# Last stage of a one-layer encoder trunk: the remaining operand splits issued in the fifth pass, and the additions of x to the u3 blocks on VectorE

## Chip, cores and metric

The kernel runs on one NeuronCore of a Trainium2 chip. The metric is the device time of one execution in microseconds; the median of several runs counts.

## What is computed

The reference is one layer of an encoder trunk on x (1024 frames of 1024 features, f32): a mixer, a SwiGLU feed-forward, and a last stage that adds a gated embedding. Only the last stage is touched by the change:

```python
h3 = rmsnorm(x, norm_ple_g[li])
x = x + jax.nn.sigmoid(h3 @ w_ple_gate[li]) * (p[li].astype(x.dtype) @ w_ple_proj[li])
```

The kernel holds everything transposed: features on the 128 partitions, frames along the free axis, in eight tiles of 128 x 1024. The embedding product `p @ w_ple_proj` was made much earlier and lies in DRAM.

## The kernel before

**Arithmetic.** Every f32 operand of a matrix product is split into a rounded part hi and a rest lo; a product is three matmuls (hi·hi, hi·lo, lo·hi). A split of a 128 x 1024 operand is an ACT copy (hi, a cast) and a subtraction on DVE (lo). Weights are split in the same way by ACT (line 123) and, in this stage, by GpSimd (POOL, line 126), which is fed by a DMA into `wr`.

**The seven passes.** The 1024 x 1024 product of the last stage, with `w_ple_gate`, is done by a Strassen scheme with seven half-size products, in the order of `KINDS`: A11, S2, A12, S3, S1, A22, S4 (lines 964 and 965 name the weight, the operand and the chain of each). A pass has four steps (`k`), and in each step 4 output blocks (`u`) of 128 x 512 take three matmuls. The passes accumulate in three chains of four PSUM banks: x (A11, A12), y (S2, S3, A22) and z (S1, S4). After a pass `after(kind, u, ps)` combines the banks. The seventh pass, S4, goes block by block instead: all its matmuls for one `u`, then `last` for that block; the fourth block is cut into two halves of 256 columns, and `last` is called for both halves after the matmuls of both have been issued, so that both waits count up to the very last matmul.

**The end of an output block.** `out(c, h, t, add)` is a stream of four parts for one block: DVE multiplies by the row factors `rb`; ACT takes the sigmoid; DVE multiplies by the embedding block `e`; and the engine `add` (GpSimd unless told otherwise) adds x, after which a DMA stores the block. `some(n)` moves streams on by one part each, so that four blocks go through a part together.

**Operand splits.** The fourteen operand tiles are split one by one with `m_split` in the order `m_order`. `operand`, called in the first and third step of a pass, takes the next split pair from `m_ready` and calls `m_split` when fewer than two are left: so the two T4 operands of the sixth pass are split during the fifth, and the two B22 operands of the seventh pass during the sixth. `side` is a generator that `passes` moves on once after each step; it holds the loads of the embedding blocks and the work on the output blocks.

**Order on an engine.** All operations through `self.V`, `self.A` and `self.G` are pinned to the order of the code on DVE, ACT and POOL; each engine takes its instructions in that order, and one that waits holds up those behind it. The weight copies (line 123) and weight rests (line 126) are not pinned: a scheduler at build time places them.

**Names.** `pm_13973` to `pm_13976` are the banks of chain z (blocks u = 0 to 3), `pm_13715` to `pm_13718` those of chain y, `s_13597` and `s_13598` hold the four u3 blocks (two in each), `s_13863` and `s_13864` the embedding blocks of the same columns, `rb_13622` the row factors. The operation that makes an output block of u3 final (fifth pass, S1) is `V.tensor_tensor(u3[u], ps, u3[u], ALU.add)`; the one beside it, `V.tensor_tensor(ps, ps, u2[u], ALU.add)`, prepares the bank for S4. The two together, for four blocks, are called the eight z additions below.

Of the kernel before, what the change touches and what calls it, by code (L numbers as in the profile page):

```python
# [56 lines left out]
class Trunk:  # L57
# [1650 lines left out]
    def ple(self):  # L1708
        nc, V, A, G = self.nc, self.V, self.A, self.G
        h0, h1 = slice(0, HALF), slice(HALF, T)  # L1710
        p1, u2, u3 = [[t[:, h] for t in (self.slot(), self.slot()) for h in (h0, h1)] for _ in range(3)]
        es = {}

        def load(odd, h):
            tiles = [self.slot() for _ in range(2)]
            for u in range(4):
                e = es[2 * u + odd, h.start] = tiles[u // 2][:, u % 2 * HALF:u % 2 * HALF + HALF]
                self.load(e, self.es[2 * u + odd][:, h])

        todo = []  # L1720

        def out(c, h, t, add=G, sp=None):

            sp = sp or slice(0, HALF)
            t, e = t[:, sp], es[c, h.start][:, sp]
            at = slice(h.start + sp.start, h.start + sp.stop)
            V.tensor_tensor(t, t, self.rb[:, at], ALU.mult)
            yield
            A.activation(t, t, AF.Sigmoid)
            yield  # L1730
            V.tensor_tensor(e, t, e, ALU.mult)
            yield
            add.tensor_tensor(e, e, self.x[c][:, at], ALU.add)
            nc.sync.dma_start(self.out[c][:, at], e)

        def some(n):

            for stream in todo[:n]:
                next(stream, None)

        def after(kind, u, ps):
            if kind == "A11":
                A.copy(p1[u], ps)
            elif kind == "S2":
                V.tensor_tensor(ps, ps, p1[u], ALU.add)
                A.copy(u2[u], ps)
            elif kind == "A12":
                todo.append(out(2 * u, h1, ps))
                next(todo[-1])
            elif kind == "S3":  # L1750
                A.copy(u3[u], ps)
            elif kind == "S1":
                V.tensor_tensor(u3[u], ps, u3[u], ALU.add)
                V.tensor_tensor(ps, ps, u2[u], ALU.add)
                todo.append(out(2 * u + 1, h0, u3[u]))
            elif kind == "A22":
                todo.append(out(2 * u + 1, h1, ps))
                next(todo[-1])
                next(todo[-1])

        def last(u, ps, sp):
            for _ in range(max(0, min(2, len(todo) - u))):
                drain(todo.pop(0))
            stream = out(2 * u, h0, ps, V, sp)
            next(stream)
            next(stream)
            todo.append(stream)
            if 0 < u < 3:
                drain(todo.pop(0))

        def operand(b, i):
            got = self.m_ready.pop(0)
            if len(self.m_ready) < 2:
                self.m_split()
            return got

        def side():
            self.half_sums(0)
            for k in range(4):
                self.square(self.x[2 * k][:, h1], 1)  # L1780
            yield
            self.half_rows(0)
            for k in range(2):
                self.ple_part("B21", k, False)
            yield
            self.half_sums(1)
            for k in range(2, 4):
                self.ple_part("B21", k, False)
            yield
            self.half_rows(1)  # L1790
            yield
            m = self.m
            load(0, h1)
            yield
            for i in range(2):
                m["T1", i] = self.slot()
                V.tensor_tensor(m["T1", i], m["B22", i], m["T2", i], ALU.subtract)
                yield
            yield

            for i in range(2):
                V.tensor_tensor(m["T2", i], m["B21", i], m["T2", i], ALU.subtract)
                m["T4", i] = m["T2", i]
                yield
            load(1, h0)
            yield
            yield
            for i in range(4):
                some(4)
                yield  # L1810
            del todo[:]

            load(1, h1)
            for i in range(4):
                yield
            load(0, h0)
            for i in range(4):
                some(4)
                if i == 3:
                    del todo[:4]  # L1820
                yield

        yield from self.passes(4, operand, after, side(), last)
        while todo:
            drain(todo.pop(0))
# [94 lines left out]
def drain(stream):  # L1920
    while True:
        try:
            next(stream)
        except StopIteration as e:
            return e.value
# [114 lines left out]
```

## Time and profile before

| | us |
|---|---|
| three runs | 1594.68, 1595.65, 1601.39 |
| median | 1595.65 |
| the profiled execution, its time | 1595.63 |
| its span, first to last instruction | 1593.7 |
| PE busy in the span | 1566.2 (98%) |
| DVE busy | 1171.8 (74%) |
| POOL busy | 783.6 (49%) |
| ACT busy | 643.7 (40%) |

PE is TensorE's matmul row, DVE is VectorE, ACT is ScalarE, POOL is GpSimd, SP is the engine that issues the DMAs. The mean granted TensorE clock was 0.998. The profiled execution lies within 0.02 us of the median, and its time is 1.93 us above its span. Instructions of a queue overlap: an instruction's duration is longer than the distance to the start of the next one, so that the distance between starts (called the pitch below) is what one instruction costs a busy queue. Times in the rows are counted from the start of the span.

### The profile page before, as it was taken

What the parts mean: (1) busy time and instruction counts of PE and PEld (TensorE: products, weight loads), DVE (VectorE), ACT (ScalarE), POOL (GpSimd) and SP (SyncE); (2) the same over time, 40 slices, a digit from 0 to 9 for tenths busy, and PEclk for the clock granted to TensorE, in tenths of its full rate; (3) what the DMA queues carried; (4) which work ended last, traced back from release to release, by engine and by line L of the source; (5) the groups of instructions that cost most, each with busy time, mean ns of one, the idle gap of its engine ahead of it and who ended that gap; (6) DMA issues with size and microseconds to landing.
All of it is one profiled execution on the core that took longest, in us unless ns stands there. A gap on an engine that the chain in (4) does not pass through costs nothing.

```text
span 1593.7 us, 21834 instructions
## 1 busy us (share of the span) xinstructions
PE 1566.2 (98%) x8224; PEld 1309.3 (82%) x8224; DVE 1171.8 (74%) x1767; ACT 643.7 (40%) x1089; POOL 783.6 (49%) x445
## 2 busy tenths in 40 slices
PE   8999999999999999999999999999999999999997
PEld 6998989877888888888887788888888888888886
DVE  5656765489998777544898988888888866765658
ACT  5321221167677633421377322232222234445453
POOL 3422221257563064325230777777777764644554
PEclk9999999999999999999999999999999999999999
DMA  5101100245663465475244422233333268875334
GB/s 191 54 28 41 40 28 27 100 146 174 224 245 107 143 192 187 146 285 210 80 141 177 152 99 99 100 99 109 103 108 108 80 255 322 304 278 189 126 134 157
DMA packets 81897, 230.52 MB, mean 145 GB/s; under 512 B 9216, under 2 KB 9984, under 8 KB 81280
## 3 DMA queue, kind: packets, MB, share of 16 engines
q1 hardware_dynamic: 81648, 229.12, 40.6%
q8 instruction: 64, 1.05, 0.2%
q14 instruction: 41, 0.34, 0.1%
q10 hardware_dynamic: 144, 0.02, 0.0%
HBM read 163.82 MB, written 65.27 MB: 144 GB/s over the span
## 4 chain that ended last, share of the span: by engine, by line
PE 80%; DVE 9%; POOL 2%; ACT 2%; issue 2%; DMA 1%; SPq 0%; POOLq 0%; ACTq 0%; DVEq 0%
PE pm L83 77%; DVE s L54 5%; PE pm L86 2%; DVE m L54 2%; ACT s L54 1%; POOL wl L126 1%; POOL m L556 1%; DVE q L54 0%; DVE wl L126 0%; ACT wh L123 0%; DVE pm L54 0%; DMA d<-s 0%; DMA s<-in_oq 0%; POOL s L1075 0%; DMA wr<-d 0%
## 5 line engine op out<-in xcount | busy, mean ns | idle before, releaser
L83 PE MATMUL pm<-s,wh 128*128 128x512 f32 (+1 forms) x1712 | 532.1, 392 | 6.7 <-ACT wh L123 5.2
L83 PE MATMUL pm<-s,whi 128*128 128x512 f32 x1568 | 488.1, 392 | 1.2 <-DVE t L54 1.2
L126 POOL TENSOR_TENSOR wl<-wr,wh 128x1024 fp32r<-128x1024 f32 (+2 forms) x108 | 265.0, 2460 | 395.9 <-ACT wh L123 392.6
L83 PEld LDWEIGHTS pm<-s,wh 128*128 128x128 f32 x1712 | 320.1, 189 | 73.7 <-ACT wh L123 5.2
L83 PEld LDWEIGHTS pm<-s,whi 128*128 128x128 f32 x1568 | 294.7, 188 | 67.0 <-DVE t L54 1.7
L83 PE MATMUL pm<-s,wl 128*128 128x512 f32 (+1 forms) x856 | 334.1, 390 | 0.0
L54 DVE TENSOR_TENSOR s<-s,s 128x512 f32<-128x512 f32 (+4 forms) x213 | 257.3, 1236 | 90.5 <-ACT s L54 53.1
L83 PE MATMUL pm<-s,wlo 128*128 128x512 f32 x784 | 307.9, 393 | 0.9 <-DVE wlo L54 0.5
L83 PE MATMUL pm<-wh,s 128*128 128x256 f32 (+1 forms) x896 | 238.2, 340 | 0.0
L123 ACT CAST wh<-wr 128x1024 fp32r<-128x1024 f32 (+2 forms) x114 | 114.8, 1008 | 268.5 <-PE pm L83 143.9
L83 PEld LDWEIGHTS pm<-s,wl 128*128 128x128 f32 x856 | 161.5, 189 | 34.2 <-POOL wl L126 0.6
L83 PEld LDWEIGHTS pm<-s,wlo 128*128 128x128 f32 x784 | 147.4, 188 | 35.0 <-DVE wlo L54 1.1
L83 PEld LDWEIGHTS pm<-wh,s 128*128 128x128 f32 x896 | 154.6, 190 | 13.9 <-DVE s L341 0.2
L54 DVE TENSOR_TENSOR t<-pm,t 128x512 f32<-128x512 f32 x138 | 94.8, 687 | 88.3 <-PE pm L83 81.9
L54 DVE TENSOR_TENSOR s<-pm,s 128x512 f32<-128x512 f32 (+1 forms) x134 | 87.0, 680 | 86.4 <-PE pm L83 86.2
L83 PE MATMUL pm<-wl,s 128*128 128x256 f32 (+1 forms) x448 | 147.5, 329 | 0.4 <-POOL wl L126 0.4
L54 POOL TENSOR_TENSOR wlo<-wr,whi 128x512 fp32r<-128x512 f32 (+1 forms) x53 | 107.5, 2037 | 74.9 <-ACT whi L54 74.1
L54 ACT CAST whi<-q 128x512 fp32r<-128x512 f32 (+1 forms) x81 | 61.4, 757 | 153.4 <-DVE q L54 131.3
L54 POOL TENSOR_TENSOR s<-s,t 128x512 f32<-128x512 f32 x44 | 76.8, 1745 | 86.7 <-ACT t L54 86.7
L54 ACT CAST s<-s 128x1024 fp32r<-128x1024 f32 (+1 forms) x94 | 90.2, 980 | 61.8 <-DVE s L54 31.9
L54 POOL TENSOR_TENSOR wlo<-q,whi 128x512 fp32r<-128x512 f32 x52 | 87.9, 1691 | 45.7 <-ACT whi L54 31.9
L83 PEld LDWEIGHTS pm<-wl,s 128*128 128x128 f32 x448 | 85.3, 191 | 5.9 <-POOL wl L126 0.6
(147 smaller groups left out, 1949.2 us busy)
## 6 DMA issues: line engine op xcount, KB each, us to landing
d<-s SPq DMA_DIRECT2D x147, 256.0 KB, 3.4
s<-d SPq DMA_DIRECT2D x67, 512.0 KB, 5.9
wr<-d SPq DMA_DIRECT2D x36, 512.0 KB, 4.0
s<-in_wq SPq DMA_DIRECT2D x22, 512.0 KB, 5.4
wr<-in_sg SPq DMA_DIRECT2D x22, 512.0 KB, 3.9
wr<-in_su SPq DMA_DIRECT2D x22, 512.0 KB, 3.8
s<-in_x SPq DMA_DIRECT2D x21, 512.0 KB, 8.0
d<-s SPq DMA_DIRECT2D x18, 512.0 KB, 6.1
```

The source lines that it names most:

```text
L54: return lambda *a, **k: self.trunk.order(op(*a, **k), self.key)
L83: return self.order(self.nc.tensor.matmul(*a, **k))
L86: return self.order(self.nc.tensor.transpose(*a, **k))
L123: self.nc.scalar.copy(hi[:, c], raw[:, c])
L126: rest.tensor_tensor(lo[:, c], raw[:, c], f32(hi[:, c]), ALU.subtract)
L556: nc.gpsimd.tensor_tensor(ss, ss, self.mhalf[:, 0:8], ALU.pow)
```

## The change

Two places differ. In `side`, the four steps of the fifth pass that were empty now each call `m_split` before they yield: three of the calls find an operand left to split, the fourth finds none. In `after`, the streams of the u3 blocks are made with VectorE as the adding engine in place of GpSimd.

```diff
             elif kind == "S1":
                 V.tensor_tensor(u3[u], ps, u3[u], ALU.add)
                 V.tensor_tensor(ps, ps, u2[u], ALU.add)
-                todo.append(out(2 * u + 1, h0, u3[u]))
+                todo.append(out(2 * u + 1, h0, u3[u], V))
...
             load(1, h1)
             for i in range(4):
+                self.m_split()
                 yield
```

On DVE, around the end of the fifth pass (`s_14024`, `s_14006`: rest of the second T4 operand; `s_14022`, `s_14044`: rests of the two B22 operands; then the z additions begin):

```order
 L54 TENSOR_TENSOR s_13934<-s_13783,s_13933 128x1024
 L54 TENSOR_TENSOR s_13984<-s_13161,s_13983 128x1024
-L54 TENSOR_TENSOR s_14024<-s_13240,s_14023 128x1024
+L54 TENSOR_TENSOR s_14006<-s_13240,s_14005 128x1024
+L54 TENSOR_TENSOR s_14022<-s_12964,s_14021 128x1024
+L54 TENSOR_TENSOR s_14044<-s_13048,s_14043 128x1024
 L54 TENSOR_TENSOR s_13597<-pm_13973,s_13597 128x512
 L54 TENSOR_TENSOR pm_13973<-pm_13973,s_13595 128x512
```

Two splits have come ahead of the eight z additions. On DVE again, from the last z addition to the first operation on the blocks of the sixth pass (`s_14066`, `s_14108` are the same two rests as before the change; `s_12023`, `s_12074`, `s_12115`, `s_12164` are tiles of x):

```order
 L54 TENSOR_TENSOR pm_13976<-pm_13976,s_13596 128x512
-L54 TENSOR_TENSOR s_14066<-s_12964,s_14065 128x1024
 L54 TENSOR_TENSOR s_13597<-s_13597,rb_13622 128x512 x2
 L54 TENSOR_TENSOR s_13598<-s_13598,rb_13622 128x512 x2
-L54 TENSOR_TENSOR s_14108<-s_13048,s_14107 128x1024
 L54 TENSOR_TENSOR s_13863<-s_13597,s_13863 128x512 x2
 L54 TENSOR_TENSOR s_13864<-s_13598,s_13864 128x512 x2
+L54 TENSOR_TENSOR s_13863<-s_13863,s_12023 128x512
+L54 TENSOR_TENSOR s_13863<-s_13863,s_12074 128x512
+L54 TENSOR_TENSOR s_13864<-s_13864,s_12115 128x512
+L54 TENSOR_TENSOR s_13864<-s_13864,s_12164 128x512
 L54 TENSOR_TENSOR pm_13715<-pm_13715,rb_13622 128x512
```

The two splits have gone from this stretch, and the four additions of x have come in, ahead of the blocks of the sixth pass; the same four rows have left POOL's queue, where they stood behind the last two weight rests. On ACT, the casts of the same operands and the last two weight casts (`wh`), which stand ahead of the sigmoids:

```order
 L54 COPY s_13983<-s_13161 128x1024
-L54 COPY s_14023<-s_13240 128x1024
-L54 COPY s_14065<-s_12964 128x1024
-L123 COPY wh_14018<-wr_14019 128x1024
-L123 COPY wh_14060<-wr_14061 128x1024
+L54 COPY s_14005<-s_13240 128x1024
+L54 COPY s_14021<-s_12964 128x1024
+L54 COPY s_14043<-s_13048 128x1024
+L123 COPY wh_14026<-wr_14027 128x1024
+L123 COPY wh_14068<-wr_14069 128x1024
 L54 ACTIVATE s_13597<-s_13597 128x512 x2
 L54 ACTIVATE s_13598<-s_13598 128x512 x2
```

The cast of the second B22 operand, which stood behind the four sigmoids, now stands ahead of both weight casts. TensorE's order is the same in both programs, and so is the order of the DMAs on SP.

## Prediction

> **What bounds the kernel now.** I read the page's chain first, then busy time by stretch, then the chain of waits near its end, then each queue in order of time.
>
> ```profile
> PE 80%; DVE 9%; POOL 2%; ACT 2%; issue 2%; DMA 1%; SPq 0%; POOLq 0%; ACTq 0%; DVEq 0%
> ```
>
> TensorE carries four fifths of the chain; the change leaves its instructions alone. The chain of waits (start, length, engine) shows where it leaves TensorE:
>
> ```profile
> 1509.69 50.00 PE pm L83 x231
> ...
> 1559.71 0.69 DVE s L54
> ...
> 1564.59 3.69 DVE s L54 x2
> ...
> 1568.30 3.39 ACT s L54 x5
> ...
> 1571.71 0.95 DVE s L54
> ...
> 1572.86 4.70 DVE s L54 x4
> 1577.55 1.29 DVE pm L54 x3
> ...
> 1590.57 0.42 DVE s L54
> ```
>
> From 1559.71 to the last operation at 1590.57, DVE sets the end, with one stretch on ACT. Busy time in the two parts of this tail:
>
> ```profile
> core 0: us, PE busy (x) PEld busy (x) DVE busy (x) ACT busy (x) POOL busy (x), PEclk, DMA share, GB/s
> ...
> 1559.70:1577.40 17.70, 17.70 (x79) 14.64 (x78) 16.06 (x18) 5.49 (x7) 8.54 (x5) 1.00 0.28 110
> 1577.40:1591.00 13.60, 6.22 (x39) 5.45 (x37) 12.99 (x24) 4.81 (x9) 8.02 (x6) 0.88 0.50 193
> ```
>
> DVE is busy 16.06 of 17.70 us, then 12.99 of 13.60, while TensorE stops 6.22 us into the second part. So the end is DVE's backlog, and a microsecond taken out of its queue counts until TensorE's last matmul is again the later of the two. DVE's queue in order of time:
>
> ```profile
> 1559.71 0.69 DVE L54 TENSOR_TENSOR s<-pm,s 128x512 f32<-128x512 f32 x1 [0.96 <-PE pm L83]
> ...
> 1563.90 0.69 DVE L54 TENSOR_TENSOR pm<-pm,s 128x512 f32<-128x512 f32 x1
> 1564.50 3.17 DVE L54 TENSOR_TENSOR s<-s,s 128x1024 fp32r<-128x1024 f32 x1
> 1567.59 2.48 DVE L54 TENSOR_TENSOR s<-s,rb 128x512 f32<-128x512 f32 x4
> 1571.71 5.84 DVE L54 TENSOR_TENSOR s<-s,s 128x1024 fp32r<-128x1024 f32 x5 [1.64 <-ACT s L54]
> 1577.48 2.48 DVE L54 TENSOR_TENSOR pm<-pm,rb 128x512 f32<-128x512 f32 x4
> ...
> 1584.88 0.69 DVE L54 TENSOR_TENSOR pm<-pm,rb 128x512 f32<-128x512 f32 x1
> ...
> 1586.80 0.42 DVE L54 TENSOR_TENSOR pm<-pm,rb 128x256 f32<-128x256 f32 x1
> 1587.66 0.43 DVE L54 TENSOR_TENSOR pm<-pm,rb 128x256 f32<-128x256 f32 x1 [0.43 <-ACT pm L54]
> ...
> 1590.57 0.42 DVE L54 TENSOR_TENSOR s<-s,s 128x256 f32<-128x256 f32 x1
> ```
>
> The eight z additions run from 1559.71 to 1564.50 (pitch 0.60). Then comes a split (1564.50), four row multiplications of u3 (1567.59), a wait of 1.64 for ACT, a second split (1571.71) and four multiplications by the embedding (from 1572.86 by the chain). At 1577.48 DVE begins on the sixth pass's blocks. From 1559.71 to there: 4.79 + 3.09 + 2.48 + 1.64 + 1.15 + 4.62 = 17.77 us. Against this, POOL's and ACT's rows:
>
> ```profile
> 1551.77 4.76 POOL L126 TENSOR_TENSOR wl<-wr,wh 128x1024 fp32r<-128x1024 f32 x2
> 1561.82 4.76 POOL L126 TENSOR_TENSOR wl<-wr,wh 128x1024 fp32r<-128x1024 f32 x2 [5.29 <-ACT wh L123]
> 1573.62 6.35 POOL L54 TENSOR_TENSOR s<-s,s 128x512 f32<-128x512 f32 x4 [7.03 <-DVE s L54]
> ```
>
> ```profile
> 1554.22 2.95 ACT L54 CAST s<-s 128x1024 fp32r<-128x1024 f32 x3
> 1560.69 1.05 ACT L123 CAST wh<-wr 128x1024 fp32r<-128x1024 f32 x1 [3.52 <-DMA wr<-d]
> 1562.00 1.05 ACT L123 CAST wh<-wr 128x1024 fp32r<-128x1024 f32 x1 [0.25 <-DMA wr<-d]
> ...
> 1570.65 1.03 ACT L54 CAST s<-s 128x1024 fp32r<-128x1024 f32 x1
> ```
>
> **Part 1, the splits leave the tail.** They cost 3.09 and 1.15 us of DVE's queue there, and the wait of 1.64 ends when the cast of 1570.65 is done: 5.88 us in all. Now they stand ahead of the z additions, behind these two:
>
> ```profile
> 1555.31 2.30 DVE L54 TENSOR_TENSOR s<-s,s 128x1024 fp32r<-128x1024 f32 x1 [8.27 <-ACT s L54]
> ...
> 1557.53 1.21 DVE L54 TENSOR_TENSOR s<-s,s 128x1024 fp32r<-128x1024 f32 x1
> ```
>
> POOL is idle from 1556.53 (1551.77 + 4.76) to 1561.82, so I take the moved splits at the pitch of the free split, 1.15 (1571.71 to 1572.86). They run from 1558.68 and 1559.83, and DVE reaches the z additions at 1560.98, not 1559.71: 1.27 lost. The bounds are 1.15 and 3.17 each; 1.15 stands nearest, since the free row of 1557.53 is their neighbour. The added cast on ACT goes behind three with a pitch of 0.95, from 1557.07 to 1558.12: DVE needs it at 1559.83, and ACT's next work waits for a DMA until 1560.69. It costs nothing; without that wait it would push the weight casts by 0.95.
>
> The z additions then last to 1565.77. TensorE needs their banks for S4:
>
> ```profile
> 1572.43 0.61 PE L83 MATMUL pm<-s,wh 128*128 128x512 f32 x2
> ...
> 1580.36 0.39 PE L83 MATMUL pm<-s,wl 128*128 128x512 f32 x1
> ...
> 1583.34 0.28 PE L83 MATMUL pm<-s,wl 128*128 128x256 f32 x1
> ```
>
> S4 is 36 matmuls of 512 columns up to 1580.59, at 0.227 each, so it starts at 1572.43, 6.7 us after the additions: TensorE doesn't notice. Its operands are ready sooner than before.
>
> **Part 2, the row multiplications.** At 1565.77 POOL is still on its second weight rest, until 1566.58. The split of 1564.50 lasted 3.17, and 1.09 of that after POOL's end, nearly a whole free split of 1.21: beside POOL an operation with two SBUF inputs hardly advanced, while the z additions, with one input in PSUM, kept their 0.69 beside it. So I let the first multiplication wait 0.81, to 1566.58; bounds are 0 and 0.81. Four at a pitch of 0.60 end at 1568.98.
>
> The sigmoid that the next step wants has this row:
>
> ```profile
> L54 ACT ACTIVATE s<-s 128x512 f32<-128x512 f32 x4 | 2.4, 634 | 5.2 <-DVE s L54 5.2
> ```
>
> The first is done by about 1566.58 + 0.68 + 0.63 = 1567.89, over a microsecond before DVE asks at 1568.98. The wait for ACT is gone and nothing is late in its place.
>
> **Part 3, x added by DVE.** Four additions come into DVE's queue ahead of 1577.48. No row before shows them on DVE with POOL idle; the bounds are 0.60, the pitch of the row multiplications, also SBUF only, and 1.79, the slowest operation of this shape:
>
> ```profile
> 1575.76 1.79 DVE L54 TENSOR_TENSOR s<-s,s 128x512 f32<-128x512 f32 x1
> ```
>
> That one ran beside POOL's additions of 1573.62, the ones removed. With them gone POOL has nothing to do here until the sixth pass's blocks come, so I take 0.60, or 2.40 for four. For the same reason the multiplications by the embedding fall from 4.62 to 2.40. The two nearly cancel: 2.40 paid, 2.22 saved.
>
> **Sum.** From 1559.71: 1.27 delay, 4.79 z additions, 0.81 wait, 2.40 row multiplications, 2.40 embedding, 2.40 additions: 14.07 us, against 17.77. DVE is 3.70 us earlier at the sixth pass's blocks (1573.78), whose last matmuls end within the three microseconds ahead of S4's start at 1572.43. From there the order is the same, so everything slides by 3.70 until it meets TensorE. The third S4 block's row multiplication goes from 1584.88 to 1581.18; its last matmul ends at 1580.36 + 0.39 = 1580.75, so it is free. The fourth block's goes from 1586.80 to 1583.10, but the program lets it wait for the last matmul of all, which ends at 1583.62. It starts at about 1583.65: 3.15 earlier than before, and 0.55 of the gain is turned into a wait for TensorE. What follows, 1586.80 to the span's end at 1593.7, is unchanged. So the span is 1590.55, and the time 1595.63 - 3.15 = 1592.5 us. The profiled execution's 1595.63 is the median but for 0.02, so I don't shift it. That is 0.2% faster; 0.5%, about what a measurement of this kernel can tell from no change, would be 8 us.
>
> **Rivals.**
>
> - **DVE stays late because the relief doesn't come.** If the embedding multiplications are slow for a reason of their own, they keep 4.62; the saving shrinks by 2.22 to 1.48, DVE stays the bound, and the time is 1594.15. For it: the four took 4.62 together, and nothing before shows them without POOL. Against: the row multiplications, same shape and sources, needed 0.60 as soon as POOL was idle. The Trainium skill speaks against this part of the change in "Perfetto Trace Analysis", section "Optimizing Scalar/DVE Operations": where VectorE is saturated, work should go off to ScalarE or even GpSimd; it adds that between VectorE and GpSimd this might not help, as they share a read port. By its first half the additions are a plain loss, which is this rival's time; by its second half, my sum. The row of 1575.76 beside POOL's of 1573.62 is for the second.
> - **TensorE's end doesn't hold DVE.** Matmul ends are modelled; if the bank is free 0.55 earlier, the whole 3.70 counts: 1591.9.
> - **Slower: GpSimd's weight rests move onto the moved splits.** They follow the casts, which wait for DMAs landing at 1560.69 and 1562.00. If the weights land some 3 us sooner, POOL's 4.76 us lie on DVE's two moved splits, which then cost 3.17 each as at 1564.50: 4.04 more than in my sum. This decides from the point at which DVE loses over 3.70, since that is all the slack it has gained: the fourth block's multiplication comes at 1587.14, 0.34 later than before, and the time is 1596.0. Against it: the order of the DMAs ahead of these loads hasn't changed.
> - **It does nothing.** Were the splits held up where they stand now by a buffer, the old times would remain, 1595.6. The order of the built program shows them moved, with waits only for their casts and for older work.
>
> **Chances.** Forecast 0.70, relief missing 0.14, TensorE's end not holding 0.06, slower by POOL 0.06, nothing 0.04. The range runs from 1591.9 less 0.97, the distance of the two nearer runs before, to the slower rival: 1590.9 to 1596.0. It holds all five cases but for run-to-run variation; one of three runs before stood 5.7 us high. No case reaches 8 us either way, so within 0.5% has 0.94, and 0.03 is left on each side for runs like that one.
>
> **What would show it.** In the changed profile: splits ending near 1561 and the first z addition near 1560.98; no wait for ACT between the row and the embedding multiplications; eight operations at a pitch of 0.60 from 1568.98; POOL idle from 1566.58 to about 1577; the first block of the sixth pass near 1573.8; and a new wait of DVE for TensorE, of about half a microsecond, ahead of the first 128x256 operation. The forecast is wrong if that wait is absent or that operation starts after 1584.2, if the eight operations take 1 us or more each, or if TensorE shows a gap ahead of S4.

## Result and profile after

| | before | changed |
|---|---|---|
| median of 22 runs each, us | 1595.59 (1593.27 to 1601.39) | 1592.51 (1589.84 to 1595.14) |
| ratio, 95% interval | | 0.998 [0.9974, 0.9986] |
| profiled execution: time, span | 1595.63, 1593.7 | 1594.29, 1592.5 |
| end of the last matmul | 1583.62 | 1585.58 |
| tail: last matmul's end to the span's end | 10.08 | 6.92 |

The gain is 3.08 us between the medians: 0.2%, with an interval of the ratio that excludes 1. The spans of the two profiled executions differ by only 1.2, since the one of the changed kernel came 1.96 later to its last matmul. That was lost long before the changed instructions: in the chain of waits up to 1500 us, a long stretch of TensorE starts 2.07 later. Before and after the change:

```profile
527.81 234.74 PE pm L83 x1040
```

```profile
529.88 234.54 PE pm L83 x1040
```

So the tail (from the end of the last matmul to the end of the span) is what is compared below; the front part differs from execution to execution by more than the change moves. In the changed kernel the chain of waits stays with TensorE to the very end:

```profile
1511.66 73.94 PE pm L83 x348
...
1585.62 0.45 DVE pm L54
...
1589.39 0.42 DVE s L54
```

It left TensorE at 1559.71 before; now it leaves for DVE at 1585.62, and only the chain of the last block is left to DVE. Busy time in the stretches shown for before:

```profile
1559.70:1577.40 17.70, 17.70 (x80) 14.66 (x79) 17.70 (x26) 5.62 (x9) 4.78 (x2) 1.00 0.46 176
1577.40:1591.00 13.60, 8.18 (x48) 7.08 (x46) 11.57 (x21) 4.09 (x8) 5.51 (x4) 0.92 0.42 161
```

DVE (the third time) has no gap left in the first stretch. POOL (the last before the clock) works 4.78 us there instead of 8.54: the two weight rests, no additions. These stretches are counted from the span's start, as they were before, so in the changed trace they lie 1.96 us earlier against TensorE's end. DVE's queue:

```profile
1557.23 5.75 DVE L54 TENSOR_TENSOR s<-s,s 128x1024 fp32r<-128x1024 f32 x4 [8.24 <-ACT s L54]
1562.91 0.68 DVE L54 TENSOR_TENSOR s<-pm,s 128x512 f32<-128x512 f32 x1
...
1567.70 3.51 DVE L54 TENSOR_TENSOR s<-s,rb 128x512 f32<-128x512 f32 x4
1571.13 4.89 DVE L54 TENSOR_TENSOR s<-s,s 128x512 f32<-128x512 f32 x8
1575.95 2.48 DVE L54 TENSOR_TENSOR pm<-pm,rb 128x512 f32<-128x512 f32 x4
...
1585.62 0.43 DVE L54 TENSOR_TENSOR pm<-pm,rb 128x256 f32<-128x256 f32 x1 [0.24 <-PE pm L83]
```

All four splits stand ahead of the z additions. The wait of 1.64 for ACT is gone, the eight operations of embedding and x run at a pitch of 0.60 (1571.13 to 1575.95), and there is a new wait, 0.24 for TensorE, ahead of the last block. POOL's rests, and ACT's casts ahead of them:

```profile
1564.08 4.78 POOL L126 TENSOR_TENSOR wl<-wr,wh 128x1024 fp32r<-128x1024 f32 x2 [5.58 <-ACT wh L123]
```

```profile
1556.15 3.90 ACT L54 CAST s<-s 128x1024 fp32r<-128x1024 f32 x4
1562.94 1.05 ACT L123 CAST wh<-wr 128x1024 fp32r<-128x1024 f32 x1 [2.89 <-DMA wr<-d]
```

After the four casts ACT still waits 2.89 for the weights' DMA, so the added cast pushes nothing back.

### The profile page after: what moved, and what is told of

Read it like the earlier page. It is cut to its first block, busy times and chain, and to the rows that moved or that the text cites. A ratio compares the mean times of both kernels' runs of the same rounds, so it can differ in the third digit from the quotient of the medians.

```text
span 1592.5 us, 21839 instructions
## 1 busy us (share of the span) xinstructions
PE 1568.6 (98%) x8224; PEld 1310.9 (82%) x8224; DVE 1169.4 (73%) x1771; ACT 644.1 (40%) x1089; POOL 779.3 (49%) x441
## 3 DMA queue, kind: packets, MB, share of 16 engines
q8 instruction: 64, 1.05, 0.3%
## 4 chain that ended last, share of the span: by engine, by line
PE 81%; DVE 8%; POOL 2%; issue 1%; DMA 1%; ACT 1%; POOLq 0%; DVEq 0%; ACTq 0%; SPq 0%
PE pm L83 79%; DVE s L54 4%; DVE m L54 2%; PE pm L86 2%; POOL wl L126 1%; POOL m L556 1%; ACT s L54 1%; DVE q L54 0%; DVE wl L126 0%; ACT wh L123 0%; DMA d<-s 0%; DMA s<-in_oq 0%; DVE wlo L54 0%; POOL s L1075 0%; DMA wr<-d 0%
```

## Experiments

My theory was that DVE's backlog fell by 3.7 us, all of it by the moved splits, and that TensorE's last matmul cut the gain to about 3.15. The rivals: that the additions on VectorE earn their share, and that DVE still sets the end. All kernels differ only from the fifth pass on. For each profiled execution (one per row):

| kernel | tail, us | DVE at the last block, against TensorE's end | POOL's first rest, after the first z addition | row multiplications of u3 |
|---|---|---|---|---|
| before | 10.08 | 3.18 late | 2.11 | 2.48 |
| the change | 6.92 | waits 0.24 | 1.17 | 3.43 |
| the change, second profile | 6.89 | waits 0.85 | 0.08 | 2.58 |
| splits alone | 6.98 | waits 0.86 | 0.78 | 3.03 |
| additions alone | 10.45 | 3.55 late | 2.28 | 2.49 |
| no additions to u3 | 6.95 | waits 0.66 | 1.95 | 4.21 |
| last block whole | 7.32 | 1.05 late | 2.45 | 4.61 |
| weights first | 7.78 | 0.90 late | 4.16 ahead | 2.41 |
| four more additions | 9.78 | 2.87 late | 1.94 | 4.22 |
| one split moved | 9.73 | 2.87 late | 2.77 | 4.95 |
| splits, weights first, whole block | 6.48 | 0.21 late | 3.89 ahead | 2.41 |
| splits, whole block | 6.46 | 0.18 late | 1.70 | 3.96 |

Times of the last column run from the first multiplication to the operation behind the fourth (to the end of the fourth where a wait follows). Free, they take 2.41.

### Each half of the change alone

```diff
-                todo.append(out(2 * u + 1, h0, u3[u], V))
+                todo.append(out(2 * u + 1, h0, u3[u]))
```

> The splits are moved as in the change, x is added to the u3 blocks by GpSimd as before. Measure: the tail, from the end of the last matmul to the span's end (10.1 us before, 6.9 with the change), since the time ahead of it varies from run to run. Theory (the moved splits free DVE, and TensorE's end then holds it): the four multiplications by the embedding run beside GpSimd's additions again, about 4.6 us instead of 2.4, but four additions of 2.4 are gone from DVE, so DVE reaches the sixth pass's blocks within 0.3 us of the full change, the tail is 6.9 to 7.0 and the time that of the change, 1592.5. Rival (the additions on DVE bring about half, by the contention they take away): tail about 8.5, time about 1594.

Measured: median 1591.89, ratio 0.9977 [0.9968, 0.9986], tail 6.98. DVE's queue (first fence) and POOL's (second):

```profile
1565.31 3.11 DVE L54 TENSOR_TENSOR s<-s,rb 128x512 f32<-128x512 f32 x4
1568.34 4.68 DVE L54 TENSOR_TENSOR s<-s,s 128x512 f32<-128x512 f32 x4
1572.95 2.48 DVE L54 TENSOR_TENSOR pm<-pm,rb 128x512 f32<-128x512 f32 x4
...
1583.26 0.43 DVE L54 TENSOR_TENSOR pm<-pm,rb 128x256 f32<-128x256 f32 x1 [0.86 <-PE pm L83]
```

```profile
1569.10 6.33 POOL L54 TENSOR_TENSOR s<-s,s 128x512 f32<-128x512 f32 x4 [3.04 <-DVE s L54]
```

Four operations beside POOL's additions take 4.61, against 4.82 for eight with POOL idle: what the second edit adds to DVE's queue and what it relieves cancel but for 0.2. The tail is the change's (6.98 against 6.92), so the moved splits carry the whole gain. The other half, on the kernel before:

```diff
-                todo.append(out(2 * u + 1, h0, u3[u]))
+                todo.append(out(2 * u + 1, h0, u3[u], V))
```

> The splits stand as before, x is added to the u3 blocks by VectorE. Theory: 2.4 us of additions paid, 2.2 of contention saved, so DVE is 0.2 us later than before, tail 10.1 to 10.4, time as before, 1595.6. Rival (the additions bring about half): tail about 8.5, time about 1594. If the contention is not what slows the embedding multiplications: they keep 4.6 us, tail 12.5, time 1598.

Measured: median 1595.22, ratio 0.9995 [0.9986, 1.0005], tail 10.45.

```profile
1565.43 3.34 DVE L54 TENSOR_TENSOR s<-s,s 128x1024 fp32r<-128x1024 f32 x1
1568.70 2.49 DVE L54 TENSOR_TENSOR s<-s,rb 128x512 f32<-128x512 f32 x4
1572.82 6.04 DVE L54 TENSOR_TENSOR s<-s,s 128x1024 fp32r<-128x1024 f32 x9 [1.64 <-ACT s L54]
1578.78 2.48 DVE L54 TENSOR_TENSOR pm<-pm,rb 128x512 f32<-128x512 f32 x4
```

The long split, the wait of 1.64 and the second split are all back, and nine operations take 5.96 where five took 5.77: no gain, as expected (the tail came out 0.05 above the range). Both rivals on the additions fall: that they bring half, and that the embedding multiplications stay slow.

### Is it TensorE that holds DVE?

This kernel leaves out the additions of x to the u3 blocks:

```diff
-                todo.append(out(2 * u + 1, h0, u3[u], V))
+                todo.append(out(2 * u + 1, h0, u3[u], None))
...
-            add.tensor_tensor(e, e, self.x[c][:, at], ALU.add)
+            if add is not None:
+                add.tensor_tensor(e, e, self.x[c][:, at], ALU.add)
```

> The change, without the additions of x to the four u3 blocks on any engine (these blocks are stored without x). Theory (TensorE's last matmul holds DVE): DVE has 2.4 us less to do and waits as much longer ahead of the last block's multiplication (wait 0.24 in the changed kernel, 2.6 here); tail 6.9, time as the change, 1592.5. Rival (DVE's queue still sets the end): tail 4.5 to 5, time 1590.1.

Measured: median 1591.42, ratio 0.9969 [0.9958, 0.998], tail 6.95: with four operations less, the tail is no shorter.

```profile
1565.23 4.28 DVE L54 TENSOR_TENSOR s<-s,rb 128x512 f32<-128x512 f32 x4
1569.44 2.49 DVE L54 TENSOR_TENSOR s<-s,s 128x512 f32<-128x512 f32 x4
...
1577.60 0.70 DVE L54 TENSOR_TENSOR pm<-pm,rb 128x512 f32<-128x512 f32 x1 [0.29 <-PE pm L83]
...
1578.92 1.68 DVE L54 TENSOR_TENSOR s<-s,s 128x512 f32<-128x512 f32 x1
...
1583.19 0.43 DVE L54 TENSOR_TENSOR pm<-pm,rb 128x256 f32<-128x256 f32 x1 [0.66 <-PE pm L83]
```

```profile
1578.75 1.30 POOL L54 TENSOR_TENSOR s<-s,s 128x512 f32<-128x512 f32 x1
```

The size of the wait was wrong: 0.66 and 0.29, not 2.6. Of the 2.40 saved, 0.78 went to slower row multiplications (4.21 against 3.43, the rests came later), and 0.87 to an addition of 1.68 instead of 0.81. It began 0.17 after POOL's addition of 1578.75 and ended 0.55 after it; in the changed kernel the same one, at 1582.64, met only the last 0.26 of a POOL addition. The rest, about 0.7, is the two waits, less the 0.24 of the change. So DVE does wait for TensorE, but for less than forecast, as work taken out also moves what follows against POOL. The other side, four useless additions more:

```diff
             add.tensor_tensor(e, e, self.x[c][:, at], ALU.add)
+            if add is V and h is h0 and c % 2:
+                V.tensor_tensor(p1[c // 2], p1[c // 2], self.x[c][:, at], ALU.add)
```

> The change, with four more additions of the same shape on DVE beside the four of x (into blocks that nobody reads any more). Theory: DVE has 0.2 to 0.6 us of slack against TensorE's end and nothing more; four additions with GpSimd idle cost 0.60 each, 2.4 in all, so the tail is 6.9 + 2.4 - 0.24 = 9.1 (8.7 to 9.2), the wait for TensorE is gone and the time is 1594.6. Rival (slack elsewhere, the stores or ACT hold the end): tail under 8. If additions cost what they did beside GpSimd, 1.2 to 1.8: tail 11.5 to 14.

Measured: median 1595.49, ratio 0.9996 [0.9987, 1.0005], tail 9.78.

```profile
1569.55 7.30 DVE L54 TENSOR_TENSOR s<-s,s 128x512 f32<-128x512 f32 x12
1576.77 2.48 DVE L54 TENSOR_TENSOR pm<-pm,rb 128x512 f32<-128x512 f32 x4
...
1586.09 0.42 DVE L54 TENSOR_TENSOR pm<-pm,rb 128x256 f32<-128x256 f32 x1
```

Twelve operations take 7.22, 0.60 each; the wait for TensorE is gone and DVE is 2.87 late: 2.40 more, less the wait of 0.24, and some 0.8 again from later rests, which puts the tail above my 9.2. So DVE's slack was under a microsecond in these executions, and work beyond it counts in full.

### One of the two splits

```diff
             for i in range(4):
-                self.m_split()
+                if i < 2:
+                    self.m_split()
                 yield
```

> The change, with only the first of the two B22 splits moved into the fifth pass; the second stays behind the row multiplications, its cast behind the four sigmoids. Theory, from the rows of before: z additions end at 1564.6, the row multiplications at about 1569, then the wait for the cast (1.6 to 1.8) and the split (1.15) come back, eight operations of 0.60 follow: the sixth pass's blocks at about 1576.6 in the time of before, 0.8 to 0.9 earlier than before and 2.8 later than the change; tail about 9.2, time 1594.7. Rival (the long split of 3.1 is what counts, the wait is filled by other work): tail 7 to 7.5.

Measured: median 1594.76, ratio 0.9993 [0.9983, 1.0002], tail 9.73.

```profile
1565.66 4.95 DVE L54 TENSOR_TENSOR s<-s,rb 128x512 f32<-128x512 f32 x4
1572.24 6.05 DVE L54 TENSOR_TENSOR s<-s,s 128x1024 fp32r<-128x1024 f32 x9 [1.64 <-ACT s L54]
1578.20 2.49 DVE L54 TENSOR_TENSOR pm<-pm,rb 128x512 f32<-128x512 f32 x4
```

The theory's account holds and the rival (tail 7 to 7.5) falls. Moving the long split alone shortens this tail by only 0.35, and the time can't be told from that of before: its 3.1 us were mostly time blocked by POOL's rests, and the row multiplications, now standing there, are blocked in its place (4.95 instead of 2.41). The wait of 1.64 and the short split, which the change also removes, make up 2.8 us. The rests came later here than in any other profile (2.77), so part of the 0.8 to 0.9 forecast may be hidden by that; this execution can't say how much.

### Where the weight rests fall

```diff
-            load(1, h1)
             for i in range(4):
                 self.m_split()
                 yield
+            load(1, h1)
             load(0, h0)
```

> The change, with the loads of the embedding blocks for the sixth pass's columns moved from the start of the fifth pass's steps to those of the sixth, so that on SP the two weight loads of S4 stand ahead of them. In the runs so far GpSimd's two weight rests, which follow these loads, began 0.8 to 2.5 us after the first z addition, and the row multiplications of u3 took 3.0 to 4.6 us instead of 2.4. Theory (the rests block DVE's operations with two SBUF inputs; TensorE's end holds the rest): the weights are asked for some 1.5 us sooner, the rests end under the z additions, the row multiplications take 2.4 to 2.6; DVE gains 1 us or more, which becomes wait for TensorE (over 1 us); tail 6.9, time as the change, 1592.5. Rival (the slower rival of the prediction): the rests now lie on the two moved splits, which take up to 3.2 each; DVE is up to 4 us late and the tail 7 to 10.

Measured: median 1593.79, ratio 0.9996 [0.9986, 1.0006], tail 7.78. DVE first, then POOL:

```profile
1551.98 8.07 DVE L54 TENSOR_TENSOR s<-s,s 128x1024 fp32r<-128x1024 f32 x4 [8.13 <-ACT s L54]
1559.97 0.68 DVE L54 TENSOR_TENSOR s<-pm,s 128x512 f32<-128x512 f32 x1
...
1564.75 2.48 DVE L54 TENSOR_TENSOR s<-s,rb 128x512 f32<-128x512 f32 x4
```

```profile
1555.81 3.15 POOL L126 TENSOR_TENSOR wl<-wr,wh 128x1024 fp32r<-128x1024 f32 x1 [2.46 <-ACT wh L123]
1559.49 2.82 POOL L126 TENSOR_TENSOR wl<-wr,wh 128x1024 fp32r<-128x1024 f32 x1 [0.54 <-ACT wh L123]
```

My theory for this run missed (no wait for TensorE, a tail above 6.9), and its rival holds. It is the mechanism of the prediction's slower rival, brought about by the edit: the first rest lies on the splits, which take 8.07 instead of 5.75. The row multiplications, now free, give back 1.0. DVE is 0.90 late at the last block: a longer tail than the change's, a shorter one than before. The interval of the ratio reaches 1, so the times alone don't tell this kernel from the one before.

### A shorter end

```diff
-                    cuts = (0, HALF) if u < 3 else (0, HALF // 2, HALF)
+                    cuts = (0, HALF)
```

> The change, with the fourth block of S4 not cut into halves: matmuls of 512 columns and one operation in place of two at each step. Theory: since both halves wait for the last matmul anyway, cutting brings nothing, and the chain behind it loses a DVE-ACT round trip: multiplication 0.68, then DVE does the third block's two operations (1.3) while ACT takes the sigmoid (0.58), then 0.6 and 0.7; the last operation ends 3.3 us after the last matmul instead of 4.2, the store is 256 KB instead of 128 (some 0.2 more): tail about 6.2, and TensorE ends 0.16 sooner; time 0.9 below the change, about 1591.6. Rival (halves overlap DVE and ACT, so cutting pays): tail 7.4 or more, time 1593 or more.

Measured: median 1591.34, ratio 0.9974 [0.9963, 0.9984], tail 7.32.

```profile
1563.84 4.69 DVE L54 TENSOR_TENSOR s<-s,rb 128x512 f32<-128x512 f32 x4
...
1582.63 0.69 DVE L54 TENSOR_TENSOR pm<-pm,rb 128x512 f32<-128x512 f32 x1
...
1585.27 0.69 DVE L54 TENSOR_TENSOR s<-s,s 128x512 f32<-128x512 f32 x1
```

The chain of the last block is 3.33 (1582.63 to 1585.96), against 4.19 with halves, as expected. But it began 1.05 after TensorE's end, since the row multiplications took 4.61 in this execution: the tail came out at 7.32, not 6.2. So two more kernels combine this edit with the splits alone (additions on GpSimd), the first of them with the weights first as well; their edits are those above.

> Splits moved as in the change, x added to the u3 blocks by GpSimd, the weight loads of S4 ahead of the embedding loads, and the fourth block of S4 whole. Theory: DVE is early enough (splits alone left a wait of 0.86 for TensorE, the earlier rests add about 1), TensorE ends 0.16 sooner, and the chain behind it is 3.3 us instead of 4.2: tail 6.2, time 0.9 below the change, 1591.3 to 1591.6. Rival: DVE is late as in the run with the whole block alone, tail 7 or more, time no better than the change.

> Splits moved as in the change, x added to the u3 blocks by GpSimd as before, the fourth block of S4 whole, loads as in the change. Theory: splits alone left DVE a wait of 0.86 us for TensorE's end, so with the whole block DVE is still there in time, or late by at most 0.3, the chain behind the last matmul is 3.3 us instead of 4.2 and the last store some 0.2 longer: tail 6.2 to 6.5, time 0.6 to 0.9 below splits alone on the same chip. If the weight rests come as late as in the run of the whole block (2.4 us after the first z addition): tail 7 to 7.4. Rival (halves pay): tail over 7.4 with a wait for TensorE in front.

Measured: 1591.92, 0.9975 [0.9966, 0.9984], tail 6.48; and 1591.46, 0.9968 [0.9955, 0.998], tail 6.46. The second met its expectation (DVE 0.18 late). The first did not: the earlier rests lie on the splits again, which take 7.81, and DVE is 0.21 late.

```profile
1556.17 7.81 DVE L54 TENSOR_TENSOR s<-s,s 128x1024 fp32r<-128x1024 f32 x4 [8.38 <-ACT s L54]
```

The changed kernel on the chip of the second:

> The changed kernel as it is, to stand beside the former on the same chip. Theory: tail 6.9 when DVE waits for TensorE's end, up to 7.4 when the weight rests come late (their start over 2 us after the first z addition); time 0.2% below before.

Measured: 1590.55, 0.9964 [0.9952, 0.9977], tail 6.89. DVE's queue there:

```profile
1566.44 2.66 DVE L54 TENSOR_TENSOR s<-s,rb 128x512 f32<-128x512 f32 x4
...
1584.35 0.43 DVE L54 TENSOR_TENSOR pm<-pm,rb 128x256 f32<-128x256 f32 x1 [0.85 <-PE pm L83]
```

With the whole block and the additions on GpSimd the tail is 0.43 shorter than here (0.52 shorter than with the splits alone) in one profile each, which the times don't resolve: no kernel here is shown to beat the change.

## Why the prediction was right

The forecast of 1592.5 met a median of 1592.51. To hit it so exactly is luck: the interval of the ratio allows a gain of 2.2 to 4.1 us, and in the five runs of the repeat the medians differ by 6.0, more than the tail's 3.2 accounts for (where the rest of that lies stays open). What carries the prediction is its steps, here in the time frame of before (subtract 1.96, the difference between the ends of the last matmul, from the changed trace):

- **First z addition**: forecast 1560.98, measured 1560.95. The added cast cost nothing.
- **Row multiplications**: forecast to end at 1568.98, measured 1569.17.
- **Eight operations**: forecast 4.80, measured 4.82. The additions cost what the vanished contention gave back, as both halves alone show; the rival of relief that doesn't come is out. The Trainium skill, "Perfetto Trace Analysis", section "Optimizing Scalar/DVE Operations", says only that offloading from a saturated VectorE may make sense, and that between VectorE and GpSimd it might not help; the 4.61 against 4.82 agree with the latter.
- **Sixth pass's blocks**: forecast 1573.78, measured 1573.99.
- **TensorE's end**: forecast a wait of 0.55, measured 0.24 and, in the second profile, 0.85. The last block's first operation was forecast at 1583.65 and measured at 1583.66. The tail fell by 3.16 (forecast 3.15); the kernel without the additions shows that less work on DVE brings no more.

Mis-sized was one term: the 0.81 that the row multiplications lose to POOL's rests, which I called an upper bound. It came from one execution; the changed one lost 1.02. In the runs with both splits moved and the order of loads unchanged, the loss was 0.2 to 2.2 us (2.58 and 4.61, against 2.41 free). That the total came out exactly owes something to the profiled case lying in the part of this spread where TensorE still hides it; with the rests 1 us later DVE would have ended the kernel late, as in the run with the whole block. The slower rival had the right mechanism and too high a price: 2.3 us on the splits, not 4.04, as the second rest falls almost wholly under the z additions, which it doesn't slow. It also left out what moved rests give back, 1.0 at the row multiplications.

That moving the first split of the two brings little was not in the prediction: it charged that split 3.09 and let the row multiplications lose only 0.81 in its place. For both together the sum held.

## What to carry to other kernels

Where DVE's queue outlasts TensorE, take work out until it waits for the last matmul, and no further: beyond that point less work in the queue gains nothing, and what is left is the chain behind that matmul. An operation that looks long because another engine blocks it is not worth its length: what takes its place is blocked too, so move it only together with the wait behind it, or see that the blocker falls under operations fed from PSUM. That happened unforced in the second profile of the change (rests 0.08 after the first z addition, row multiplications 2.58); the two kernels that load the weights first put a rest on the splits instead. Handing additions from GpSimd to a full DVE was neutral here, since they blocked about as much as they cost.

## What the runs showed of the hardware

A 128x512 operation of DVE with both inputs in SBUF took 0.60 us of its queue alone, and the z additions, one input in PSUM, kept 0.60 in every run, beside GpSimd too. An operation with both inputs in SBUF that began while GpSimd was at work ended a fixed time after GpSimd's operation: 0.55 to 0.59 for 128x512 (1580.60 against 1580.05 in the kernel without additions), 1.08 to 1.09 for a 128x1024 split (1567.67 against 1566.58 before the change). This holds from 1548 us on in all twelve profiles, but for two embedding multiplications of the run with splits, weights first and whole block, where GpSimd's addition was the one held up (2.9 us instead of 1.3). So the length of such an operation says how much of GpSimd's was left: up to 2.9 for a row multiplication in the run with one split moved. Where DVE's operation was first, GpSimd's could be the longer, as there or in the run with the weights first (3.15 instead of 2.4).

With both splits moved and the order of loads unchanged, the casts that follow the weight loads let POOL start 0.08 to 2.45 us after the first z addition; what makes the landing vary was not tried.
